# Softmax on one core: one row of one load is issued as thirteen DMAs over few partitions

## The chip, the cores and the metric

The kernel runs on one core of a Trainium2 chip. The metric is device time in microseconds of one execution. Before the change the median of 12 runs is 162.72 us (162.22 to 164.1).

## What is computed

A softmax over the last axis with temperature 2, in float32:

```python
x: (16, 1024, 512) float32
x_scaled = x / 2.0
x_max = np.max(x_scaled, axis=-1, keepdims=True)
exp_x = np.exp(x_scaled - x_max)
out = exp_x / np.sum(exp_x, axis=-1, keepdims=True)
```

33.55 MB are read and 33.55 MB written.

## The kernel before

The input is seen as 16,384 vectors of 512 numbers. They are cut into ten tiles (PLAN, L11): a tile has r "rows", which means r vectors in each of the 128 partitions, and the vectors of one partition lie next to each other in DRAM. A row of a tile is thus 2,048 bytes in each partition. The tiles have 3, 5, 9, 15, 21, 23, 23, 15, 11 and 3 rows (128 in all) and are computed in chunks of 3 to 8 rows. Everything stays in one SBUF buffer, the arena of 99 rows; tiles 0 to 6 fill it, and tiles 7 to 9 take over the places of tiles 0 to 3 once those have been stored (`behind`, L75 to L80).

For each chunk, VectorE takes the negated maximum (`do_max`, L123), which waits for the whole tile's load; ScalarE takes exp row by row, in place, and sums it (L158); VectorE takes the reciprocal of the sums and multiplies (`do_mul`, L132), with one instruction for a chunk in tiles 3 and 4 (FUSED, L138) and one a row elsewhere (L145). VectorE's order is written out: the maximum of chunk k, then the multiply of chunk k - 2 (LAG, L173).

All transfers are issued by SyncE (SP) on one queue, in the order of QUEUE (L21): loads 0 to 6, stores 0 to 4, loads 7 to 9, stores 5 to 9. The first load is put ahead of the program's start-up barrier (EARLY). A store waits on SP for the multiply of its tile's last chunk (L100), a load into a place in use waits for the stores from there (L116). A transfer adds 16 to its semaphore when it has landed, and `loads_of` (L92) counts how much of that a tile's load makes. An entry of QUEUE can name a range of rows and a list of partition groups (first, end, step); `do_queue` (L108) then issues one DMA for each group. Before the change no entry does.

Of the kernel before, what the change touches and what calls it, by code (L numbers as in the profile page):

```python
# [18 lines left out]


QUEUE = [  # L21
    ("load", 0), ("load", 1), ("load", 2), ("load", 3), ("load", 4), ("load", 5), ("load", 6),
    ("store", 0), ("store", 1), ("store", 2), ("store", 3), ("store", 4),
    ("load", 7), ("load", 8), ("load", 9), ("store", 5), ("store", 6), ("store", 7),
    ("store", 8), ("store", 9),
# [207 lines left out]
```

## Time and profile before

| what | value |
|---|---|
| median of 12 runs | 162.72 us (162.22 to 164.1) |
| the profiled execution's own time | 163.33 us |
| its span | 161.5 us |
| VectorE busy | 130.3 us (81%) |
| ScalarE busy | 94.0 us (58%) |
| DMA, mean over the span | 416 GB/s |
| load 3 (15 rows, 3,840 KB), landed | 22.30 us |
| last multiply ends | 141.09 us |
| last store landed | 160.48 us |

The profile is of one execution. Its span is the time between the first and the last instruction that it records; the execution's time has some 1.8 us around that. Busy times are sums for each engine, which work beside each other. A DMA consists of packets that 16 DMA engines move; in this trace a full transfer has eight data packets for each engine, one for each partition, and one packet of 4 bytes that counts the semaphore up. The queue named q1 holds the program's transfers, q14 fetches of the program's own instructions.

### The profile page before, as it was taken

The page shows a single profiled execution, that of the slowest core. Times are in us where ns is not written, and L with a number is a line of the kernel's source. Part 1 is how long each engine was busy: PE and PEld are TensorE (multiplying, and loading weights), DVE is VectorE, ACT ScalarE, POOL GpSimd, SP SyncE. Part 2 cuts the span into 40 slices and gives each one's busy share as a digit, 9 for nine tenths or more (in the row PEclk, how much of TensorE's full clock was granted, in tenths as well). Part 3 has the DMA queues.
Part 4 walks back from the last instruction along what each step waited for, and adds up shares of the span by engine and source line. Part 5 has one row for each costly group of instructions (what it writes and reads, how often), then busy time and mean ns, then how long its engine had stood idle before and what let it go on. Part 6 is the DMA issues. An engine that isn't in the chain of part 4 may idle for free.

```text
span 161.5 us, 465 instructions
## 1 busy us (share of the span) xinstructions
DVE 130.3 (81%) x142; ACT 94.0 (58%) x257; POOL 0.2 (0%) x4
## 2 busy tenths in 40 slices
DVE  0567989999999999999999999979999999900000
ACT  3455957674759583939494959848547789000000
POOL 0000000000000000000000000000000000000000
DMA  7999989998998996999999999999999999999991
GB/s 258 453 441 415 472 379 501 417 468 385 478 443 385 467 420 243 446 438 458 418 463 447 405 429 428 423 441 431 428 455 443 408 432 455 390 434 431 411 412 73
DMA packets 2883, 67.13 MB, mean 416 GB/s; under 512 B 320, under 2 KB 320, under 8 KB 832
## 3 DMA queue, kind: packets, MB, share of 16 engines
q1 hardware_dynamic: 2880, 67.11, 97.6%
q14 instruction: 3, 0.02, 0.0%
HBM read 33.55 MB, written 33.55 MB: 415 GB/s over the span
## 4 chain that ended last, share of the span: by engine, by line
DVE 54%; DMA 31%; SPq 1%; issue 0%; DVEq 0%
DMA arena<-in_x_dram 31%; DVE negmax L125 27%; DVE arena L145 13%; DVE arena L138 12%; DVE recip L134 1%; SPq L118 0%; DVEq L228 0%; SPq L103 0%; SPq L116 0%
## 5 line engine op out<-in xcount | busy, mean ns | idle before, releaser
L158 ACT ACTIVATE arena<-arena,negmax 128x512 f32<-128x512 f32 x128 | 90.7, 709 | 42.4 <-DVE negmax L125 42.4
L125 DVE TENSOR_REDUCE negmax<-arena 128x5 f32<-128x2560 f32 (+5 forms) x22 | 71.5, 3251 | 10.0 <-DMA arena<-in_x_dram 10.0
L145 DVE TENSOR_SCALAR arena<-arena,recip 128x512 f32<-128x512 f32 x92 | 37.9, 481 | 0.6
L158 ACT ACTIVATION_READ_ACCUMULATOR arena<-arena,negmax 128x1 f32 x128 | 23.9, 187 | 0.0
L138 DVE TENSOR_TENSOR arena<-arena,recip 128x2560 f32<-128x2560 f32 (+1 forms) x6 | 20.2, 3359 | 0.2
L134 DVE RECIPROCAL recip<-sums 128x5 f32<-128x5 f32 (+5 forms) x22 | 4.0, 183 | 0.0
L158 ACT ACT_TABLE_LOAD x1 | 1.3, 1283 | 0.8 <-PEq L217 0.8
L217 POOL MEMSET const-bfloat16-1.0<- 128x1 bf16 x1 | 0.1, 102 | 0.0
L217 POOL MEMSET const-uint8-127<- 128x1 uint8 x1 | 0.1, 102 | 0.0
L217 POOL MEMSET const-float32-1.0<- 128x1 f32 x1 | 0.1, 99 | 0.0
L217 POOL MEMSET const-float32-0.0<- 128x1 f32 x1 | 0.1, 98 | 0.2 <-issue 0.2
## 6 DMA issues: line engine op xcount, KB each, us to landing
arena<-in_x_dram SPq DMA_DIRECT2D x2, 5888.0 KB, 53.3
out_dram<-arena SPq DMA_DIRECT2D x2, 5888.0 KB, 28.0
arena<-in_x_dram SPq DMA_DIRECT2D x2, 3840.0 KB, 25.2
out_dram<-arena SPq DMA_DIRECT2D x2, 3840.0 KB, 25.5
arena<-in_x_dram SPq DMA_DIRECT2D x1, 5376.0 KB, 32.7
out_dram<-arena SPq DMA_DIRECT2D x1, 5376.0 KB, 20.5
arena<-in_x_dram SPq DMA_DIRECT2D x1, 2816.0 KB, 29.2
out_dram<-arena SPq DMA_DIRECT2D x1, 2816.0 KB, 18.3
```

Source lines behind the costliest of these rows:

```text
L125: nc.vector.reduce_max(out=negmax[:, b : b + c], in_=arena[:, a : a + c], axis=mybir.AxisListType.X, negate=True,)._wait_ge(ld[t], loads_o ...
L134: nc.vector.reciprocal(out=recip[:, b : b + c], in_=sums[:, b : b + c])._wait_ge(s_exp, k + 1).then_inc(s_rec, 1)
L138: nc.vector.tensor_mul(out=arena[:, a : a + c], in0=arena[:, a : a + c], in1=recip[:, b : b + c].unsqueeze(2).to_broadcast([P, c, D]),)._w ...
L145: ins = nc.vector.tensor_scalar_mul(out=arena[:, a + r], in0=arena[:, a + r], scalar1=recip[:, b + r : b + r + 1],)
L158: ins = nc.scalar.activation(out=arena[:, a + r], in_=arena[:, a + r], func=mybir.ActivationFunctionType.Exp, bias=negmax[:, b + r : b + r ...
L217: nc = _bacc.Bacc("TRN2", target_bir_lowering=False, num_devices=1)
```

## The change

Load 3 stood in the queue as one DMA of 15 rows over 128 partitions. It becomes one DMA of rows 0 to 13 over 128 partitions, and after it 13 DMAs that load row 14: nine that take 13 partitions each (o, o + 9, ... up to o + 108, for o = 0 to 8, together partitions 0 to 116), and four that take every fourth of partitions 117 to 127 (three, three, three and two partitions). They stand in the queue between load 3 and load 4, add to the same semaphore, and the wait for load 3 grows from 16 to 16 x 14. Nothing else is changed; the instructions of VectorE, ScalarE and GpSimd are the same in number and order.

```diff
 QUEUE = [
-    ("load", 0), ("load", 1), ("load", 2), ("load", 3), ("load", 4), ("load", 5), ("load", 6),
+    ("load", 0), ("load", 1), ("load", 2), ("load", 3, 0, 14, [(0, 128, 1)]),
+    ("load", 3, 14, 15, [(o, o + 109, 9) for o in range(9)] + [(o, 128, 4) for o in range(117, 121)]),
+    ("load", 4), ("load", 5), ("load", 6),
     ("store", 0), ("store", 1), ("store", 2), ("store", 3), ("store", 4),
```

## The prediction

> **What bounds the kernel now.** I read the slices of the page first, then the DMA queues, the stretches at the end, the waits, and last the DMA issues around the edited load. (The packet times below come from the trace's DMA packet records: I linked each packet to the one that starts where it ends, which gives 16 strings, one per DMA engine.)
>
> ```profile
> ## 2 busy tenths in 40 slices
> DVE  0567989999999999999999999979999999900000
> ACT  3455957674759583939494959848547789000000
> POOL 0000000000000000000000000000000000000000
> DMA  7999989998998996999999999999999999999991
> ...
> q1 hardware_dynamic: 2880, 67.11, 97.6%
> q14 instruction: 3, 0.02, 0.0%
> ```
>
> The DMA row is full from the first slice to the last, and VectorE is empty for the last five. The queue's packets fill 97.6% of 16 engines' span. The chain of waits would have misled: it names VectorE 54% and DMA 31%, but it ends with VectorE's last multiply (140.69 + 0.40 = 141.09 us), some 20 us before the end. All that is left then is stores that drain.
>
> ```profile
> 114.00:141.50 27.50, 26.84 (x48) 17.48 (x48) 0.00 (x0) 1.00 1.01 436
> 141.50:158.00 16.50, 0.00 (x0) 0.00 (x0) 0.00 (x0) 1.00 0.96 414
> 158.00:159.00 1.00, 0.00 (x0) 0.00 (x0) 0.00 (x0) 1.00 0.33 135
> 159.00:160.20 1.20, 0.00 (x0) 0.00 (x0) 0.00 (x0) 1.00 0.05 20
> 160.20:161.50 1.30, 0.00 (x0) 0.00 (x0) 0.00 (x0) 1.00 0.00 0
> ```
>
> The last two columns are the DMA share and GB/s. From 159.0 to 160.2 the share is 0.05: about one engine of 16 (0.0625). So the end isn't 16 engines finishing together. The packet strings agree: fifteen end between 157.7 and 159.1 us and one at 160.15 us, its last landing is at 160.48, the span ends at 161.5. The strings have hardly a gap from 1 us on, except that every engine loses about 0.9 us near 61 us, where loads turn to stores. The end is therefore **the last engine's own sum of packets**. That last engine was with the early ones at first; two of the three 8 KB instruction fetches (q14; at 29.06 and 99.25 us, 0.31 us each) fell on it and cost it about 0.6 us each with the packets they delayed, and one packet at 97.5 us took 1.72 us where 1.14 is usual. Which number this engine has, the trace doesn't say. That is the main unknown of this forecast.
>
> ```profile
> L118 SPq DMA_DIRECT2D arena<-in_x_dram x10: 333/462/905, 0.0 to 83.8; - x10
> ...
> 0.00 3.91 SPq L118 DMA_DIRECT2D arena<-in_x_dram  x7
> 17.46 58.52 SPq L103 DMA_DIRECT2D out_dram<-arena  x5
> ...
> 22.32 2.82 DVE L125 TENSOR_REDUCE negmax<-arena 128x5 f32<-128x2560 f32 x1 [0.50 <-DMA arena<-in_x_dram]
> ```
>
> SP's issue of a load takes 0.33 to 0.91 us; all first seven are out at 3.91 us, and SP then waits for VectorE until 17.46. VectorE waits 0.50 us for load 3, at 22.32.
>
> **What the change does to each engine.** Load 3 (15 rows, 30,720 B a partition) becomes 14 rows over all partitions, then the 15th row (2,048 B a partition) in 13 small DMAs. The trace shows only transfers over 128 partitions, with 16 landings each. [...] It puts one packet of each 13-partition DMA on engines 0 to 12, and the last four (3, 3, 3, 2) on 0, 1 and 2. So engines 0 and 1 get 13 packets of the row, engine 2 gets 12, engines 3 to 12 get 9, and engines 13 to 15 none, where each had 8.
>
> Prices: a 6,144 B packet takes 234 ns, a 47,104 B one 1,740 ns: 75 ns per 2,048 B plus 8 ns per packet, of which 3 overlap with the next. A small packet is thus 80 ns net, a 28,672 B packet 1,059 (30,720 B: 1,135), a semaphore packet of 4 B 6 ns net. Load 3 costs an engine now 8 x 1,135 + 6 = 9,086 ns. After:
> - engines 13 to 15: 8 x 1,059 + 6 = 8,478, so **-0.61 us**
> - engines 3 to 12: 8,478 + 9 x 86 = 9,252, **+0.17 us**
> - engine 2: 8,478 + 12 x 86 = 9,510, **+0.42 us**; engines 0 and 1: 8,478 + 13 x 86 = 9,596, **+0.51 us**.
>
> Each is carried to that engine's end, as the strings have no gap to absorb it.
>
> **The price of a small packet** is an estimate from larger ones, no row shows two semaphore packets nearer than 1.9 us on one engine. Below: 80 + 6 ns. Above: the shortest first packet on a cold engine took 362 ns for 6,144 B against 234 settled, so 128 ns more each: +1.3 us on engines 3 to 12 (0.17 + 9 x 0.128), +2.2 on 0 and 1. It can't be under the bytes' 75 ns. [...] By the row, the time from a DMA's last data through its semaphore packet to the next DMA's data is 9 ns on nearly every string, the landing following 0.33 us later beside other work[...], and load 2 is still running ahead of these. I take the row, 86 ns.
>
> **SP.** 13 more issues ahead of loads 4, 5 and 6 and store 0: 13 x 0.46 = 6.0 us (0.33 to 0.91: 4.3 to 11.8). Load 4 is then issued at about 2.4 + 6.0 = 8.4 us (at most 14.2) where load 3 lands at 21.46 to 22.30: hidden by 7 us at least. Without that cover each further us of issue would idle all engines. Store 0 is due at 17.46 and its queue place comes at 61: hidden. Extra instructions could bring one more 8 KB fetch, 0.3 to 0.6 us on one engine; at the end only if that is the last one; I take nothing.
>
> **Load 3's landing.** Its semaphore now waits for engine 0's 13th small packet: 21.98 to 22.82 us (0.51 later than the earliest or latest landing now), so VectorE starts 0 to 0.5 us later. Behind that wait is all VectorE work to 75.6 us, and ScalarE behind it, with SP behind both. The tightest place is store 4, issued at 75.64, which the engines reach at 82.25 to 83.39 when store 3 ends: 6.6 us of slack. Later stores have about 7 or more (store 7, issued at 133.25 and reached at 140.5). Cost zero; it would cost time only beyond those 6.6 us. ScalarE's 42.4 us of waits for VectorE lie beside the DMA.
>
> **The forecast and its rivals.**
>
> *A, the last engine is one of 3 to 12 (45%).* It gets one packet more and its end moves 160.15 to 160.32; engine 0 or 1, if it was the next at 159.1, ends at 159.6, still earlier. On the profiled execution: 163.33 (span 161.5 plus 1.8 around it) to 163.5; on the median, 162.72 + 0.17 = **162.9**. For it: ten of 16 engines.
>
> *B, the last engine is one of 13 to 15 (20%).* It ends at 159.54, and the next at 159.3 to 159.6: 0.55 to 0.6 us gained, 162.1 to 162.2. Against it, beside the count of 3 in 16: the packets run at 47,104 B / 1,740 ns = 27.07 GB/s[...]. [...] the extra delays of those engines at fetches (0.6 us of a string lost, later not regained) show that an engine's loss counts. I leave B most of its gain.
>
> *C, the last engine is 0, 1 or 2 (13%).* +0.42 to +0.51: 163.1 to 163.2.
>
> *D, slower: small packets are dear (22%).* Place: the rings of engines 0 to 12 at about 21 us, where each small packet brings its own completion write. If an engine doesn't overlap them as it overlaps large ones, the end moves by 1.3 us (A's engine, upper price): 164.0; up to 2.2 for engines 0 and 1. It decides from 0.17 + 9 x p = 0.81, so p = 71 ns beyond my 86. For it: nothing in the trace is as dense as this. Against it: 9 ns semaphore packets without a gap in every other place.
>
> That the edit doesn't do what it says (13 partitions spread over 16 engines, or all on one) is inside D and A: evenly spread, nothing but packets is added, about +0.1 us.
>
> **How the numbers follow.** 0.5% is 0.81 us, about what a measurement of this kernel can tell from no change; the twelve runs alone lie 162.22 to 164.1, so the last engine's lag isn't the same in each. A and C are within it, B also, though noise or a better rest of the queue takes 0.08 of it beyond: faster 0.08. Slower is D and a little of C: 0.26. The rest, 0.66, is the same. Low 162.0 takes in B; high 164.0 takes in A, C and half of D; that leaves out some 0.16.
>
> **What would show it.** The small DMAs should land with load 3; VectorE's wait for load 3 should be 0.5 to 1.0 us. Packets of 2,048 B should take 80 to 85 ns (D: 150 or more). Three engines should run 0.6 us ahead from 22 us on, two 0.5 us behind; the last stretch should show whether one engine is still alone at the end. SP's load issues should be over before 15 us. I am wrong if the DMA row shows a hole near 21 us (issue or ring), or if the end moves by over 0.8 us either way.

## The result, and the profile after

The changed kernel takes 164.24 us (median of 12 runs, 163.91 to 164.38), beside 162.79 us for the kernel before (median of 49 runs, 162.22 to 164.59): a ratio of 1.0074 with a 95% interval of 1.0052 to 1.0097, so 0.7% slower. (The ratio compares the mean times, 164.21 and 163.00 us; the medians lie further apart, 1.0089, because the runs of before lie in two bunches and their median falls into the lower one.) The runs of before spread over 2.4 us, those of the changed kernel over 0.5 us, and none of them is as short as the median of before. The profiled execution took 163.92 us, with a span of 162.1 us.

The page of the changed kernel:

```profile
DVE  0467949999999999999999999999999999900000
...
DMA  7999998999999999999999999999999999999990
...
q1 hardware_dynamic: 3136, 67.11, 97.3%
```

Still one full DMA row, with VectorE done 20 us before the end. There are 256 packets more: 128 of 2,048 B and 128 completion packets of 4 B (a completion is the write with which an engine counts the semaphore up once its part of a DMA is done). Where the time went is seen in stretches. The busy columns are VectorE, ScalarE and GpSimd, the last two the mean share of 16 DMA engines and GB/s. First the kernel before, around load 3's landing and around the turn from loads to stores:

```profile
21.50:23.50 2.00, 1.50 (x2) 1.09 (x4) 0.00 (x0) 1.00 0.94 409
61.00:62.50 1.50, 1.50 (x1) 0.00 (x0) 0.00 (x0) 1.00 0.02 8
```

Then the changed kernel, with its end:

```profile
21.50:23.50 2.00, 0.46 (x2) 1.23 (x4) 0.00 (x0) 1.00 0.71 224
61.00:62.50 1.50, 1.50 (x1) 0.72 (x3) 0.00 (x0) 1.00 0.44 188
...
141.50:158.00 16.50, 0.40 (x2) 0.00 (x0) 0.00 (x0) 1.00 0.98 421
158.00:159.00 1.00, 0.00 (x0) 0.00 (x0) 0.00 (x0) 1.00 0.31 127
159.00:160.20 1.20, 0.00 (x0) 0.00 (x0) 0.00 (x0) 1.00 0.10 41
160.20:161.50 1.30, 0.00 (x0) 0.00 (x0) 0.00 (x0) 1.00 0.02 9
```

Three things are to be seen. There is a hole at load 3 that was not there: 224 GB/s where 409 were moved. The hole at 61 us has become smaller. (A packet is counted where it starts and ends, so single short stretches swing; the packet records below do not.) And from 159 us on there are now between one and two engines at work where one was, and one of them goes on past 160.2. The last store lands at 161.07 us, 0.59 later than in the profile of before, which is just the difference of the two profiled times (163.92 - 163.33).

VectorE and SP, in the changed kernel:

```profile
24.11 2.82 DVE L127 TENSOR_REDUCE negmax<-arena 128x5 f32<-128x2560 f32 x1 [2.15 <-DMA arena<-in_x_dram]
...
L120 SPq DMA_DIRECT2D arena<-in_x_dram x23: 333/681/1135, 0.0 to 83.9; - x23
...
0.00 13.67 SPq L120 DMA_DIRECT2D arena<-in_x_dram  x20
```

VectorE's wait for load 3 grew from 0.50 to 2.15 us, and SP had its loads out at 13.67 us instead of 3.91. Neither reaches the end: store 4 is issued at 77.42 us, and the engines reach it at 82.38 to 83.48, so 5.0 us of the slack are left.

**Where each engine loses time.** The packets of a trace were linked into 16 strings as in the prediction. I took each packet's duration over the usual one for its size (84 ns for 2,048 B, 234 for 6,144, 1,589 for 43,008, 1,740 for 47,104) and any gap, by stage, as a mean over the 16 engines in us:

| kernel (profiled time) | behind load 3, 20 to 24.8 us | first turn, 59 to 64 | second turn (load 9 to store 5), 111 to 115 |
|---|---|---|---|
| before (163.33) | 0.00 | 0.96 | 0.21 |
| before again, e4 (163.62) | 0.00 | 0.91 | 0.04 |
| one DMA, e3 (162.22) | 0.00 | 0.94 | 0.08 |
| changed (163.92) | 0.78 | 0.05 | 0.43 |
| two DMAs, e1 (163.91) | 0.61 | 0.01 | 0.54 |
| eight even DMAs, e2 (162.66) | 0.70 | 0.01 | 0.38 |
| 112 and 16 partitions, e5 (163.60) | 0.71 | 0.02 | 0.45 |
| thirteen touches, e6 (164.41) | 0.72 | 0.31 | 0.41 |
| ladder of touches, e8 (164.38) | 0.66 | 0.76 | 0.08 |
| eight even touches, e9 (163.49) | 0.54 | 0.16 | 0.43 |
| spaced ladder, e10 (163.43) | 0.00 | 1.08 | 0.06 |

In the changed kernel the time is lost in load 4's first packet, which takes 1.99 to 2.53 us on every engine instead of 1.59. Of the 128 small packets before it, 111 took the 84 ns that the forecast gave them. And what is lost there is nearly all missing again at the first turn; of the kernels with an early hole, only e8 loses much at both.

### The profile page after: what moved, and what is told of

Same layout as the page of the kernel before. It is cut to its first block, busy times and chain, and to the rows that moved or that the text cites. A ratio compares the mean times of both kernels' runs of the same rounds, so it can differ in the third digit from the quotient of the medians.

```text
span 162.1 us, 478 instructions
## 1 busy us (share of the span) xinstructions
DVE 130.2 (80%) x142; ACT 93.9 (58%) x257; POOL 0.2 (0%) x4
## 4 chain that ended last, share of the span: by engine, by line
DVE 72%; DMA 8%; SPq 6%; issue 1%; DVEq 0%
DVE negmax L127 37%; DVE arena L147 21%; DVE arena L140 12%; DMA arena<-in_x_dram 8%; SPq L120 6%; DVE recip L136 1%; DVEq L230 0%
```

## The experiments

Each ratio is to runs of the kernel before made beside it; that kernel's own median there lay between 162.84 and 163.37 us. Edits that alter the line of thirteen groups are shown against the changed kernel, the others against the kernel before; they are shortened where dots or words in brackets stand. Theories: T1, completion writes that follow each other closely hold up their engine; T2, the 2,048 B packets are slow; T3, the extra load on engines 0 to 2 decides; T4, 2,048 B packets are slow where their DMA isn't over all 128 partitions ("off home" in e5's label).

**e1, two DMAs for thirteen.**

```diff
-    ("load", 3, 14, 15, [(o, o + 109, 9) for o in range(9)] + [(o, 128, 4) for o in range(117, 121)]),
+    ("load", 3, 14, 15, [(0, 117, 1), (117, 128, 1)]),
```

> Row 14 in two DMAs, over partitions 0 to 116 (13 engines, 9 packets each) and 117 to 127 (11 engines, one each), in place of thirteen: nearly the same relief of engines 13 to 15, the same 128 packets of 2,048 B, but 2 completion writes per engine at most. T1 (each completion write of a small DMA costs about 0.3 us on its engine, not overlapped): load 3 lands at 22.0 to 22.6 us as before, the time is 162.2 to 163.0. T2 (the 2,048 B packets themselves are slow): load 3 lands at about 24, the time is 164.2 as in the changed kernel. T3 (the 10 KB more on engines 0 to 2): at most 0.3 us over before, 163.0.

164.19 us, 1.0059 (1.0033 to 1.0085). Load 3 landed at 24.00 us, most of it by 22.8; load 4's first packets took 2.1 to 2.2 us on nearly all engines, the three without small packets included. T1 alone falls: two completions are enough for a hole here. T2 or T4 is left.

**e2, eight even DMAs.**

```diff
+    ("load", 3, 14, 15, [(o, 128, 8) for o in range(8)]),
```

> Row 14 in eight DMAs of 16 partitions (every eighth), so that each of 16 engines should get one packet of each: no engine is relieved or loaded, but each has 8 completion writes more. T1: the same stall behind load 3 as in the changed kernel (load 3 lands at 23.5 to 24, first packets of load 4 take 2 us and more), time 163.9 to 164.3. T2: the same. T3: none of it, 162.7 to 162.9.

163.69 us, 1.0043 (1.0007 to 1.0079); load 3 landed at 24.10 us, 0.70 us lost per engine behind it. No engine is relieved or loaded (going by e8, where a DMA over k partitions went to k engines), and the hole is there: T3 doesn't make it. The profiled execution was a short one, 162.66 us, with this hole in it and its last engine at 159.49 us: a hole of this size doesn't by itself make an execution long. The time fell between what T3 expected and what T1 and T2 did.

**e3, one DMA.**

```diff
+    ("load", 3, 14, 15, [(0, 128, 1)]),
```

> Row 14 as one DMA over 128 partitions: only the split of load 3, with 8 packets of 2,048 B per engine and one more completion write. T1: 162.7 to 162.9, load 3 lands at about 22.4. T2: load 3 lands at about 24, time 164. T3: 162.7 to 162.9.

162.95 us, 0.9982 (0.9949 to 1.0016): no difference. All 128 packets of 2,048 B took 84 ns and load 3 landed at 22.33. T2 falls: the same bytes in the same packets cost nothing when they go as one transfer over 128 partitions.

**e4, the kernel before once more.** No edit.

> The kernel before once more, for a second profile of it. Its runs lie in two bunches, near 162.7 and 163.7; the profile known is of one of 163.3, with a stretch of no traffic at 61 to 62 us and one engine 1 us behind all others at the end. Expected 162.7; if the stretch without traffic at 61 us is what parts the bunches, a profile near 162.5 lacks it; if the last engine's lag is, that engine ends with the others.

163.6 us, 1.0009 (0.9968 to 1.0049). The profile (163.62 us) has the hole at 61 us, as has e3's of 162.22; so that hole doesn't part short runs from long ones. In these three profiles the last engine does: it ended at 160.41 us here and 160.15 in the first profile, alone, and with the others at 159.03 in e3. Here it isn't the engine with two fetches (that one ended at 159.44) but one that fell 0.8 us behind by the time load 1 landed.

**e5, meant as even, but not in the form of a full transfer.**

```diff
+    ("load", 3, 14, 15, [(0, 112, 1), (112, 128, 1)]),
```

> Row 14 in two DMAs, over partitions 0 to 111 (7 packets for each of 16 engines) and 112 to 127 (one each): no engine is relieved or loaded, each has two completion writes[...]. T1 (completion writes): no stall, load 3 lands at about 22.3, the first packets of load 4 take 1.59 us, 162.3 to 163.4 like before. T3 (uneven load): the same as T1. T4[...]: the first packets of load 4 take 2.0 us and more, load 3 lands at 22.7 to 24, and the time is 0.4 to 0.7% over before.

163.48 us, 1.0030 (1.0000 to 1.0059). Load 3 landed at 24.07 us, and load 4's first packets took 1.74 to 2.39 us. e3 and e5 differ in how the 128 partitions are divided into DMAs, and in one completion. So there is a hole that comes with the division (0.71 us per engine, where e3 has 0.00), as T4 said (two completions alone should not make one: in e8 up to five did not); its price in time is at the edge of what could be measured. What in the division makes it was not shown; no record names a packet's partition.

**e6, thirteen touches: the completions without the bytes.** Load 3 is whole again, and the thirteen DMAs load 16 bytes a partition into a scratch buffer that nothing reads.

```diff
-    ("load", 3, 0, 14, [(0, 128, 1)]), ("load", 3, 14, 15, [thirteen groups]),
+    ("load", 3), ("touch", 3, 14, 15, [the same thirteen groups]),
...
+    nc.sync.dma_start(out=extra[p:q:step, n_extra[0], :], in_=dram(xf, t)[p:q:step, lo, 0:4]).then_inc(ld[t], 16)
```

> Load 3 whole as before, and behind it the thirteen DMAs of the change with 16 bytes a partition in place of 2,048, into a scratch buffer (data not used): all completion writes of the change, no bytes worth naming. T1: the full stall, load 3 lands at 23.5 to 24, first packets of load 4 2.0 us and more, 0.5 to 0.8% over before. T4 and T3: load 3 lands within 0.5 us of before, at most 22.8, first packets of load 4 at 1.6 us, no change in time beyond 0.2%.

164.40 us, 1.0092 (1.0067 to 1.0116): all of the loss, with 2 KB of data in all. Load 3's count was full at 23.75 us. Its stretches, in the columns of above:

```profile
21.00:22.00 1.00, 0.62 (x2) 1.00 (x3) 0.00 (x0) 1.00 2.29 648
22.00:23.00 1.00, 0.00 (x0) 0.38 (x2) 0.00 (x0) 1.00 0.00 0
23.00:24.00 1.00, 0.22 (x1) 0.00 (x0) 0.00 (x0) 1.00 1.49 645
```

No packet starts or ends between 22 and 23 us: every engine sits in the long first packet of load 4 or, on three engines, in a usual one. Those three had first packets of 1.59 to 1.60 us, the others 2.10 to 2.92. At the first turn the three lost 1.11, 1.12 and 1.15 us, and all others at most 0.28 us, but for one with 0.77. Thirteen small DMAs with next to no data are thus enough, as T1 said. But each touch puts a 16-byte packet together with its completion on an engine, so the touches don't part the completions from the tiny writes in front of them. The trade between hole and turn goes engine by engine. It also shows who is idle: three engines have none of the touches, as the prediction took it of 13 to 15.

**e7, the same thirteen on load 7.**

```diff
+    ("load", 3), ...
-    ("load", 7),
+    ("load", 7, 0, 14, [(0, 128, 1)]), ("load", 7, 14, 15, [the same thirteen groups]),
```

> The thirteen DMAs take the last row of load 7 (also 15 rows), behind the turn from loads to stores at 61 us, in place of load 3's. If the 0.9 us that every engine loses at 61 us in the kernel before is the place where the stall at load 3 is given back (it is missing there in the changed kernel), then here the loss at 61 us returns, the stall stands at 105 us and is not given back, and the time is at or over the changed kernel's, 0.6 to 1.2% over before. If the two have nothing to do with each other, the same 0.7% as the changed kernel.

164.97 us (4 runs), 1.0131 (1.0061 to 1.0202). The loss at the first turn is back (1.19 us per engine), and about 1.3 us per engine, fetches included, are lost from 64 to 111 us; the last small packet's completion came at 110.3 us. As the give-back said, the two now add, though with so few runs the interval still overlaps the changed kernel's.

**e8, a ladder of touches.** Fifteen touches over partitions 0 to k - 1.

```diff
+    ("load", 3), ("touch", 3, 14, 15, [(0, k, 1) for k in range(1, 16)]),
```

> Load 3 whole as before, and behind it fifteen DMAs of 16 bytes a partition over partitions 0 to k - 1, for k = 1 to 15, into a scratch buffer (data not used). If k partitions use the lowest k engines, engine number n gets 15 - n packets of 16 bytes, so that each engine's string of packets can be named by their count: which number does the engine have that fetches instructions twice and ends last? Guess from the changed kernel's strings: 13, 14 or 15. If all DMAs go over other engines, the counts will not be 0 to 15.

164.38 us, one run, so its time isn't compared; what counts is its engines side by side. The strings hold 0 to 15 touches, each number once: a touch over k partitions went to k engines, all those of the shorter touches among them. The trace gives no engine numbers, so engine n is here the one with 15 - n touches. The first packets of load 4, over 1.59 us, sorted: 1.73, 1.59, 1.30, 1.26, 1.22, 1.14, 0.94, 0.79, 0.33, 0.18, 0.01 and five times 0.00 us. Engine 0 has 15 completions, engine 1 has 14, and so on: with up to five there is next to no delay, and from 5 to 15 it grows by 1.73 / 10 = 0.17 us each on average (unevenly: 0.46 from seven to eight). All these completions add to one semaphore, yet the engines with few were not held up, so the delay goes by each engine's own count. The engine with two fetches had the second longest, 1.59 us, which puts it among the lowest numbers; my guess of 13 to 15 falls. It ended last, at 161.19 us. This run also shows how far the first turn gives a hole back: engines with up to nine touches lost 0.5 to 1.3 us at hole and turn together, whether the hole held them up or not; engines with ten to fifteen lost 1.6 to 2.9 us, because the turn cost them 0.4 to 1.3 us again.

**e9, eight even touches.** Eight touches of 16 partitions, so eight completions for each engine, going by e8.

```diff
+    ("load", 3), ("touch", 3, 14, 15, [(o, 128, 8) for o in range(8)]),
```

> Load 3 whole as before, behind it eight DMAs of 16 bytes a partition over 16 partitions each (scratch, data not used): eight completion writes on every engine, no bytes, no uneven load. If the completion writes alone set the time: load 3 lands at about 23, the first packets of load 4 take 0.4 to 0.8 us more, 163.6 to 164.4 (0.5 to 0.9% over before, as with thirteen). If what counts at the end is that engines are set apart from each other (13, 12, 9 and no completions), then the stall is there but even, and the time is at most 0.3% over before.

163.69 us, 1.0021 (0.9988 to 1.0054). VectorE waits nearly as long as with thirteen:

```profile
DVE negmax L137 <- DMA extra<-in_x_dram: 1.9, 1, 1.9
```

e6's line has 2.2 us there. But the time doesn't differ measurably from before, and the interval lies below e6's. A hole that is even over the engines seems to be given back, and one that sets engines apart not. This isn't parted from the count, though: here each engine has eight completions, in e6 ten of them have nine, three have more and three none.

**e10, the ladder spaced out.** Two or three touches behind each of loads 1 to 6.

```diff
+    ("load", 0), ("load", 1), ("touch", 1, 0, 1, [(0, 1, 1), (0, 2, 1)]), ("load", 2),
+    ("touch", 2, 0, 1, [(0, 3, 1), (0, 4, 1)]), ("load", 3), ("touch", 3, 0, 1, [(0, k, 1) for k in (5, 6, 7)]),
...
```

> Fifteen DMAs of 16 bytes over partitions 0 to k - 1, for k = 1 to 15 (scratch, data not used), but spread two or three at a time behind loads 1 to 6. The ladder behind load 3 delayed engines by about 0.15 us for each completion over four or five, and the ones with up to four not at all. If only a run of completions without data between costs, nothing is delayed here: first packets after them at their usual time, 162.2 to 163.0, within 0.2% of before. If each completion costs wherever it stands, engine 0 is 15 x 0.15 = 2.3 us late and the time 0.8 to 1.4% over. Counts of 16-byte packets per string name each engine; the one with two instruction fetches should have 13 to 15 (engine 0, 1 or 2), by the length of its first packet of load 4 in the ladder.

163.58 us, 1.0025 (0.9998 to 1.0052). All first packets of load 4 took 1.59 us, and load 3 had landed whole by 22.24 us: fifteen completions on engine 0 made no hole when they came at most three together. That is shown; the 0.25% is not told apart from nothing. These strings also settle the engine. Behind load 2 stand two touches, for engines 0 to 2 and 0 to 3. The seven packets of them are at 11.945, 11.957, 11.958, 11.965, 12.044, 12.056 and 12.191 us, the first six each 6 ns behind load 2's completion packet or the first touch's; they only pair up if the engine of the last, which is the one with the fetch at 29.31 us, had both. It is engine 0, 1 or 2.

**e11, three packets fewer on engines 0 to 2.**

```diff
-    [(o, o + 109, 9) for o in range(9)] + [(o, 128, 4) for o in range(117, 121)]
+    [(o, o + 109, 9) for o in range(9)] + [(117, 128, 1)]
```

> The change with its last four DMAs (3, 3, 3 and 2 partitions, on engines 0, 1 and 2) replaced by one over the last eleven partitions: engines 0 to 10 get ten small packets, 11 and 12 nine, so engines 0 to 2 have three fewer packets and completions, 0.25 us of packets. If the extra load on engines 0 to 2 decides, 0.2 to 0.5 us less than the changed kernel: 163.7 to 164.0. If the stall of all thirteen engines decides, 164.2 as the changed kernel.

163.85 us, 1.0039 (1.0013 to 1.0065). The hole is there (0.67 us per engine), and the time is between before and changed, as T3 expected for the end. The interval still overlaps the changed kernel's a little, so this supports that engines 0 to 2 decide, and doesn't prove it.

**e12, the thirteen on load 6.**

```diff
+    ("load", 3), ...
-    ("load", 6),
+    ("load", 6, 0, 22, [(0, 128, 1)]), ("load", 6, 22, 23, [the same thirteen groups]),
```

> The thirteen DMAs take the last row of load 6, right ahead of the turn from loads to stores at 61 us. If the stall and the loss at the turn stand in for each other, they fall together here: load 6 lands 0.5 to 1.5 us later than before, because the row is at its end, and the time is 163.5 to 164.3. If they add, store 3 lands 0.7 us or more later than the 83.4 us of before, and the time is over 164.5.

163.64 us, 1.0021 (0.9998 to 1.0043). Load 6 landed at 66.60 us instead of 63.88, but store 3's first eleven engines landed at 82.43 to 82.77, as before (82.25 to 82.91). The last landed at 85.33, which is past the mark set for "they add"; but an engine was 1.6 us late since load 1 in this run (9.23 us against 7.66), so that mark doesn't tell. The time does, and lies where "stand in for each other" put it. Hole and turn cost 0.85 us together, 0.02 at the second turn. So they seem to stand in for each other, and this place is cheaper than load 3, though its thirteen DMAs set the engines apart just as much.

No version was faster than the kernel before; e3 is equal to it.

## Why the forecast of no change failed, step by step

The forecast was 162.9 us (162.0 to 164.0), with 0.66 for no change; measured are 164.24, 0.74% over before, and the hole near 21 us that it named as a sign of being wrong is there. What happened is a mixture of rivals C and D: D's mechanism for the hole, C's engine at the end.

- **"A small packet is thus 80 ns net ... a semaphore packet of 4 B 6 ns net."** This is the step that failed. In their records both sizes are right (84 and 9 ns, less 3 of overlap). But the price of a small DMA isn't all in its own records: in e6 the last completion packet is recorded at 21.76 us and the count is full at 23.75, 2.0 us later, where 0.33 was usual. Beyond about five in a row, each further touch with its completion held its engine for 0.17 us (e8), and 9 to 13 of them cost load 4's first packet 0.5 to 1.3 us in e6. The one row that I leaned on, completion packets without a gap, was of completions at least 1.9 us apart; "no row shows two semaphore packets nearer than 1.9 us on one engine" stood in the text, and was a reason to give rival D more than 0.22.
- **"Each is carried to that engine's end, as the strings have no gap to absorb it."** Wrong, and to the good: each engine loses 0.9 us at the first turn, and an engine that was held up by less than about 1 us at load 3 loses about that much less there (e6 and e8, engine by engine; longer holds were given back in e6 but for one engine, in e8 they weren't). I had seen the 0.9 us and taken it as fixed. So a hole of 0.78 us per engine costs little by itself (e2's profile).
- **Who is last.** The forecast gave 45% to engines 3 to 12, 20% to 13 to 15, and 13% to 0 to 2. Which engines a small DMA uses was an assumption of mine; the counts bear it out (0 to 15 touches in e8, each number once; in e6 ten engines with nine, three with more, three with none). e8 and e10 put the engine with two fetches among 0 to 2, which get the most small packets. In the changed kernel that engine is last, at 160.75 us: beside the fetches it loses 1.32 us at the second turn, where it lost 0.72 before. From profile to profile its account is: +0.50 us until it begins load 4, mostly for the packets that the change gives it (C's term, forecast at +0.51); +0.89 in the hole; -0.81 at the first turn; -0.54 because the slow packet at 97.5 us didn't come again; +0.60 at the second turn. That makes +0.64, where its end moved by 0.60. In e3's short profile (162.22 us) it lost 0.02 us at the second turn and wasn't last. So the late engine of before, late only in some executions, seems to be late in all of the changed kernel's, to judge by 12 runs within 0.5 us. That the spread of the engines decides (e9 doesn't differ from before, e6 does by 0.9%) isn't shown: in e9 the same engine lost 1.14 us at the second turn as well.
- **Rival B.** Relieving engines 13 to 15 helped nothing: the end isn't theirs. Their first packets of load 4 were long too in the changed kernel (no engine under 1.99 us), while in e6, without the bytes, three were usual. So 2,048 B packets in DMAs over a part of the partitions go with a hole of their own (0.71 us in e5, 0.00 in e3), whose cause was not shown. The two holes don't add up: 0.72 us (e6), 0.71 (e5) and 0.78 (both).
- **SP.** 0.46 us an issue was forecast; a 13-partition DMA with step 9 took 0.75 us. Load 4 was issued at 12.31 us against the forecast 8.4, within the upper 14.2 and before load 3 was through; the cover held. There were three instruction fetches again, as taken.
- **Load 3's landing.** 21.98 to 22.82 us forecast, 24.09 measured, by the completions. The slack of 6.6 us at store 4 took it, as said.

Open: which small DMAs make the hole is shown (e3, e6, e10), but not the way from the hole to the later end. Why an engine held up at load 3 is spared at the first turn and loses some 0.4 us at the second, as the kernels with an early hole do (table; e8, at 0.08 us, doesn't), was not taken apart, and the 0.6 us more of the last engine there is read from one profile each. Nor was it tried to relieve engine 0, 1 or 2: every transfer over fewer partitions that was tried here loads them.

## What to carry to other kernels

When the DMA engines are the bound, find the engine that ends last and its number before moving bytes between engines; here a DMA over k < 16 partitions loaded k engines, the same first ones each time (e8: 0 to 15 packets on the 16, each number once), and the engine late by instruction fetches was one of these. Small DMAs should not come in a row: beyond about five on one engine, with 16 bytes of data each, every further one held it up by 0.17 us on average (one ladder, e8), while the same number spread two or three at a time behind large transfers made no hole (e10: load 4's first packets at their usual 1.59 us). A stall of less than about 1 us was given back here where the engines change from loads to stores; longer ones only in part (e8: up to nine touches, 0.5 to 1.3 us lost at hole and turn together; ten to fifteen, 1.6 to 2.9). Count what a stall costs at the end of the last engine, not where it stands.

## What the hardware showed that was not expected

SP took longer for DMAs over partitions with a step: 0.75 us for 13 partitions with step 9 (e6) and 0.59 for 16 with step 8 (e9), against 0.36 for 13 contiguous partitions (e8), all with 16 bytes a partition. Thirteen counts on load 3's semaphore came between 3.59 and 12.70 us in the changed kernel, one for each small issue and long before any of its data. The 16 + 128 completions make 144 of the 224 that the wait asks for, so these thirteen must bring the other 80, each the rest of its DMA's 16 (an estimate: the records don't give the size of a count). And two of the three instruction fetches in a run fell on one engine, about 0.6 us each with the packet that they delayed, in all profiles.
